# An encoder trunk on one core: the third unit of the first feed-forward layer gets two sums of weights from DRAM instead of one, and other sums are made at other times

## The chip, the core and the metric

The kernel runs on one core of one Trainium2 chip. TensorE (PE) multiplies matrices, VectorE (DVE) and ScalarE (ACT) work elementwise, GpSimd (POOL) does little here but issue adding DMAs, and SyncE (SP) issues nearly all other DMAs. The metric is the device time of one execution in microseconds (us), given as the median of several runs.

## The reference

Two layers over 256 positions of 2048 channels, all in float32. Only the feed-forward part that follows each mixer matters here:

```python
def conv_ffn(x, w_up, conv_w, conv_b, w_down):
    u = x @ w_up                                  # 2048 -> 2 * 5632, gate and value
    up = jnp.pad(u, ((0, 0), (1, 1), (0, 0)))
    u = c[0] * up[:, :-2] + c[1] * up[:, 1:-1] + c[2] * up[:, 2:] + conv_b
    gate, val = jnp.split(u, 2, axis=-1)
    return (jax.nn.silu(gate) * val) @ w_down

for layer in range(2):
    x = x + mixer(rms_norm(x))      # layer 0: pooling and attention, layer 1: mLSTM
    x = x + conv_ffn(rms_norm(x), w_up[layer], ...)
```

## The kernel before, in words

**Weights as one stream.** All weights are cut into 890 chunks of 128 x 1024 floats (512 KB), in the order in which TensorE uses them: chunks 0 to 79 for attention, 80 to 403 for the first feed-forward layer, 404 to 565 for the mLSTM layer, 566 to 889 for the second feed-forward layer. `Stream.load(i)` makes SP issue the DMA of chunk i into a buffer `w`; in a feed-forward layer it runs 7 chunks ahead of use and has 7 buffers. `Stream.split` then makes of `w` a high part, rounded by ScalarE (line 152, a cast), and a low part, the rest, by VectorE (line 153, a subtraction), both in a tile `hl`. A float32 product is three passes of TensorE: high by high, high by low, low by high. The helper that issues all of them is line 268. The order of TensorE's work is written out by hand; that of the other engines comes from a scheduler that simulates a timeline when the program is built, except for instructions that are pinned in program order.

**Units.** Of the 44 feature tiles of a feed-forward layer, 20 are made in five units of four. A unit (`quads`) multiplies with seven block products in place of eight, which needs sums of weight blocks. Call the four blocks of a pair of rows b11, b12, b22 and b21; they lie side by side in `in_q`. A unit needs b11, first = b11 + b12, second = first + b22, third = second + b21, and "left" = b12 + b22. It goes through eight pairs; each pair has two chunks early in the unit (the even one holds b11 and first, the odd one second and third) and one "left" chunk later. In `UNITS` each unit has a number that says who makes its sums:

- kind 2 (all other units): first, second and third are made in DRAM, in a tile `G`, ahead of time. SP copies b11, b22 and b21 into `G`, and POOL issues DMAs that add: b12 on b11 in two halves of 64 partitions (line 124), then first on b22 and second on b21 (line 128). SP later loads from `G`.
- kind 3 (the third unit of the first layer, before): only first is made in `G`. The odd chunk is loaded as plain b22 and b21, and VectorE makes second (line 142, `add(l, l, self.sum)`) and third (line 143, `add(r, r, l)`) in `w`, before the chunk can be split.
- "left" is made by VectorE in all of these units (line 140).

**When the sums are made.** `make_step` runs in four parts per pair, and each part hangs on the load of a chunk: `places` gives, for each pair, the chunk of part 0 and the gap between parts, so `(150 + 4 * k, 2)` puts the parts of pair k at chunks 150 + 4k, 152 + 4k and so on. Parts 0 and 1 are the two halves (SP's copies and line 124), parts 2 and 3 the two adds of line 128; kind 3 has nothing in parts 2 and 3. Five rows of `places` serve the first layer's units, and one list of 40 pairs serves the second layer's. In it `at` is 566.

A load from `G` waits on SP until the sum that it reads has landed, and holds up all loads behind it.

Of the kernel before, what the change touches and what calls it, by code (L numbers as in the profile page):

```python
# [64 lines left out]
class Stream:  # L65
# [16 lines left out]
    def load(self, pieces=1):  # L82
        i = self.n_load
        src = self.srcs[i]
        kind, src = src if isinstance(src, tuple) else ("plain", src)
        w = self.home(i, True).tile([P, CH * P], F32, tag="w", name=f"w{i}")
        if kind in ("made", "have"):
            width = n = CH * P
            at = 0
            for part in src:  # L90
                part = self.made[part[0]][:, part[1] * 512 : part[2] * 512] if isinstance(part, tuple) else part
                to = at + part.shape[-1]
                self.nc.sync.dma_start(w[:, at:to], part)
                at = to
        else:
            width = src.shape[-1]
            n = width // pieces
            for c in range(0, width, n):
                self.nc.sync.dma_start(w[:, c : c + n], src[:, c : c + n])
        self.w[i] = [w, n, width, kind, False]  # L100
        self.n_load += 1
        for step in self.make.pop(i, ()):
            self.make_step(*step)
# [7 lines left out]
    def make_step(self, key, kind, part, src):  # L111

        pin, sync, add = self.tc.keep_in_program_order, self.nc.sync, self.nc.gpsimd
        G = self.made_tile(key)
        if part < 2:
            r = slice(64 * part, 64 * part + 64)
            if kind == 1:
                pin(sync.dma_start(G[r], src[r]))
                pin(add.dma_start(G[r, 0:1024], src[r, 512:1536], accum_op=ALU.add))
            else:  # L120
                pin(sync.dma_start(G[r, 0:512], src[r, 0:512]))
                if kind == 2:
                    pin(sync.dma_start(G[r, 1024:2048], src[r, 1024:2048]))
                pin(add.dma_start(G[r, 0:512], src[r, 512:1024], accum_op=ALU.add))  # L124
        elif kind < 3:
            at = 1024 if part == 2 else 1536
            of = 0 if part == 2 else 1024
            pin(add.dma_start(G[:, at : at + 512], G[:, of : of + 512], accum_op=ALU.add))  # L128

    def sums(self, i):  # L130
        if i in self.w and not self.w[i][4] and self.w[i][3] not in ("plain", "made"):
            w, kind = self.w[i][0], self.w[i][3]
            l, r = w[:, 0:512], w[:, 512:1024]
            pin, add = self.tc.keep_in_program_order, self.nc.vector.tensor_add
            if kind == "sum":
                pin(add(r, r, l))
            if kind in ("sum", "have"):
                self.sum = r
            if kind == "left":
                pin(add(l, l, r))  # L140
            if kind == "chain":
                pin(add(l, l, self.sum))
                pin(add(r, r, l))
            self.w[i][4] = True
# [30 lines left out]
class Weave:  # L175
# [6 lines left out]
    def add(self, gen, delay=0.0):  # L182
        self.q.append([self.t + delay, gen])
# [37 lines left out]
def trunk(ctx: ExitStack, tc: tile.TileContext, gx, xT, xn, call, catt, cml, weights, make, out):  # L221
# [716 lines left out]
    def ffn_layer(layer, norm, nxt):  # L938
        with ExitStack() as es:
# [199 lines left out]
            def sums_ready():  # L1139
                yield from wv.wait(lambda: norm.R is not None)  # L1140
                v.tensor_scalar_mul(n0, norm.rcol[:, 0:1], -1.0)
                yield from sums()
# [82 lines left out]
def _down_chunks(w):  # L1225
# [6 lines left out]


UNITS = (
    ((1, 1, 17, 38, 2), (2, 1, 45, 64, 2), (3, 1, 71, 97, 3), (4, 1, 104, 127, 2), (5, 1, 134, 157, 2)),
    ((1, 1, 17, 39, 2), (2, 1, 46, 67, 2), (3, 1, 74, 97, 2), (4, 1, 104, 128, 2), (5, 1, 135, 157, 2)),
)

# [1 line left out]
def _ffn_plan(layer):  # L1240

    slots = []
    for c, n in enumerate(FCH):
        fill = [("n", c, i) for i in range(n) if not any(u[0] == c and u[1] == i // 4 for u in UNITS[layer])]
        if c:
            per = len(fill) // NB
            fill = sum(([*fill[per * b : per * b + per], ("d", c - 1, b)] for b in range(NB)), [])
            if c == 2 and any(u[:2] == (1, 1) for u in UNITS[layer]):
                fill = [fill[i] for i in (0, 2, 1, 4, 3, 6, 5, 7)]
        for e in fill:  # L1250
            slots += [e] * (4 if e[0] == "n" else FCH[e[1]] // 2)
    here = [[] for _ in slots]
    m = KT // 2
    for c, h, lo, hi, _ in UNITS[layer]:
        one, two = 2 * m, m + m // 2
        step = (hi - lo - 3) / (one + two)
        for k in range(one + two):
            here[int(lo + k * step + (3 if k >= one else 0))].append(("s", c, h))
    plan = []
    for e, extra in zip(slots, here):  # L1260
        plan += [e] + extra
    for b in range(NB):
        plan += [("d", len(FCH) - 1, b)] * (FCH[-1] // 2)
    return plan
# [15 lines left out]
def _ffn_order(layer, up, dn, four, last):  # L1280

    pos, seq = {}, []
    m = KT // 2
    d0 = [sum(FCH[:c]) // 2 * NB for c in range(len(FCH))]
    for step in _ffn_plan(layer):
        kind, c, i = step
        n = pos.get(step, 0)
        pos[step] = n + 1
        if kind == "n":
            seq.append(up[(sum(FCH[:c]) + i) * 4 + n])  # L1290
        elif kind == "d":
            seq.append(dn[d0[c] + i * (FCH[c] // 2) + n])
        else:
            u = [e[:2] for e in UNITS[layer]].index((c, i))
            made = UNITS[layer][u][4]
            if n >= 2 * m and (n - 2 * m) % 3 == 2:
                seq.append(last[u, (n - 2 * m) // 3])
                continue
            at = n // 2 if n < 2 * m else (n - 2 * m) // 3 * 2 + (n - 2 * m) % 3
            q, key = four[u, at], f"{layer}{c}{i}_{at}"  # L1300
            if n >= 2 * m:
                seq.append(("made", ((key, 1, 2), q[:, 1024:1536])) if made == 1 else ("left", q[:, 512:1536]))
            elif n % 2:
                seq.append(("made", ((key, 2, 4),)) if made in (1, 2) else ("chain", q[:, 1024:2048]))
            else:
                seq.append((("made", "have")[made == 3], (q[:, 0:512], (key, 0, 1))) if made else ("sum", q[:, 0:1024]))
    return seq
# [124 lines left out]
```

## Time and profile before

| | us |
|---|---|
| median of 3 runs | 2164.64 (2164.61 to 2164.88) |
| the profiled execution | 2164.07 |
| its span, first to last instruction | 2162.3 |
| PE busy | 2155.0 |
| DVE busy | 1716.1 |
| ACT busy | 1308.5 |
| POOL busy | 276.0 |

The mean granted TensorE clock is 0.999 of full speed, and the DMAs move 276 GB/s on average. A row of the profile names the line, the engine, the tile written and those read, a count, the busy time and the mean of one; a row of the waits names who waited, for what, the sum in us, how often, and the longest one. A row of the timeline gives start and duration in us, and in brackets the idle time before it with what ended it. SPq stands for the issuing of DMAs by SP.

### The profile page before, as it was taken

How to read it: one execution, taken by the hardware profiler on the slowest of the kernel's cores; microseconds unless marked ns; L12 is line 12 of the kernel's file. 1: busy time of each engine (PE TensorE's matmuls, PEld its weight loads, DVE VectorE, ACT ScalarE, POOL GpSimd, SP SyncE). 2: the span in 40 equal slices, each digit the busy share in tenths (PEclk: the TensorE clock that was granted, in tenths of full speed). 3: DMA queues.
4: the chain of work that ended last, by engine and by line, in shares of the span. 5: the costliest groups of instructions: out<-in, count | busy, mean ns of one | idle time of the engine just before them, and what ended most of it. 6: DMA issues, size and time to landing. Idle time of an engine off the chain costs nothing.

```text
span 2162.3 us, 31058 instructions
## 1 busy us (share of the span) xinstructions
PE 2155.0 (100%) x10896; PEld 1827.3 (85%) x10896; DVE 1716.1 (79%) x2400; ACT 1308.5 (61%) x1840; POOL 276.0 (13%) x344
## 2 busy tenths in 40 slices
PE   9999999999999999999999999999999999999999
PEld 7888888888888888889888888888888888888887
DVE  7686698989888797866777676669898888879785
ACT  7665566766556576656554544456676666757663
POOL 0222111211111111101111111110000000000000
PEclk9999999999999999999999999999999999999999
DMA  9878899999999999979899988877999999877773
GB/s 327 256 226 247 253 262 329 336 329 315 311 328 297 360 312 348 315 207 249 250 268 247 259 249 247 259 243 223 312 284 309 301 294 291 272 253 235 260 244 119
DMA packets 204702, 596.15 MB, mean 276 GB/s; under 512 B 26010, under 2 KB 28354, under 8 KB 204546
## 3 DMA queue, kind: packets, MB, share of 16 engines
q1 hardware_dynamic: 167776, 531.43, 70.1%
q0 software_dynamic: 33696, 59.00, 18.6%
q10 hardware_dynamic: 3074, 3.75, 0.9%
q8 instruction: 85, 1.39, 0.2%
q14 instruction: 71, 0.58, 0.1%
HBM read 591.93 MB, written 119.58 MB: 329 GB/s over the span
## 4 chain that ended last, share of the span: by engine, by line
PE 99%; DVE 1%; issue 0%; ACT 0%; DVEq 0%; ACTq 0%
PE up L268 25%; PE dn L268 21%; PE p L268 17%; PE op L268 8%; PE mv L268 4%; PE mk L268 4%; PE mq L268 4%; PE mo L268 4%; PE qproj L268 3%; PE kproj L268 1%; PE pool L268 1%; PE vproj L268 1%; PE tr L1081 1%; PE av L268 1%; PE qk L268 1%; PE end L268 1%
## 5 line engine op out<-in xcount | busy, mean ns | idle before, releaser
L153 DVE TENSOR_TENSOR hl<-w,hl 128x1024 fp32r<-128x1024 f32 (+2 forms) x892 | 1074.0, 1217 | 323.0 <-ACT hl L152 309.0
L152 ACT CAST hl<-w 128x1024 fp32r<-128x1024 f32 (+2 forms) x891 | 923.5, 1048 | 641.3 <-PE dn L268 105.0
L268 PE MATMUL up<-xx,hl 128*128 128x512 f32 (+1 forms) x3072 | 560.7, 337 | 0.0
L268 PEld LDWEIGHTS up<-xx,hl 128*128 128x128 f32 x3072 | 486.8, 188 | 76.7
L268 PE MATMUL dn<-hl,g 128*128 128x512 f32 x2064 | 492.0, 391 | 0.0
L268 PEld LDWEIGHTS dn<-hl,g 128*128 128x128 f32 x2064 | 386.1, 188 | 79.4
L268 PE MATMUL p<-hl,sx 128*128 128x512 f32 x960 | 250.4, 390 | 1.9 <-DVE hl L153 1.9
L124 POOL DMA_DIRECT2D G<-in_q x160 | 132.1, 827 | 881.0 <-DMA G<-in_q 877.4
L268 PEld LDWEIGHTS p<-hl,sx 128*128 128x128 f32 x960 | 175.9, 188 | 36.6 <-DVE hl L153 2.9
L128 POOL DMA_DIRECT2D G<-G x144 | 127.3, 884 | 530.7 <-DMA G<-in_q 228.2
L268 PE MATMUL p<-hl,xx 128*128 128x512 f32 x720 | 193.7, 391 | 0.0
L268 PEld LDWEIGHTS p<-hl,xx 128*128 128x128 f32 x720 | 131.1, 188 | 24.2
L268 PE MATMUL mk<-xx,hl 128*128 128x512 f32 (+1 forms) x512 | 92.5, 338 | 0.0
L268 PE MATMUL mq<-xx,hl 128*128 128x512 f32 (+1 forms) x512 | 92.2, 337 | 0.0
L268 PE MATMUL mv<-hl,xx 128*128 128x512 f32 (+2 forms) x480 | 91.7, 350 | 0.0
L268 PE MATMUL op<-hl,cat 128*128 128x512 f32 x384 | 91.6, 393 | 0.0
L268 PE MATMUL mo<-hl,xx 128*128 128x512 f32 x384 | 90.5, 391 | 0.0
L268 PE MATMUL op<-hl,mcat 128*128 128x512 f32 x384 | 89.5, 392 | 0.0
L268 PEld LDWEIGHTS mq<-xx,hl 128*128 128x128 f32 x512 | 79.3, 188 | 11.6
L268 PEld LDWEIGHTS mk<-xx,hl 128*128 128x128 f32 x512 | 79.0, 188 | 11.7 <-DVE hl L153 0.4
L268 PEld LDWEIGHTS mv<-hl,xx 128*128 128x128 f32 x480 | 78.3, 189 | 11.2
L268 PEld LDWEIGHTS op<-hl,mcat 128*128 128x128 f32 x384 | 71.5, 188 | 14.6
(242 smaller groups left out, 1861.5 us busy)
## 6 DMA issues: line engine op xcount, KB each, us to landing
w<-in_up SPq DMA_DIRECT2D x192, 512.0 KB, 6.2
w<-in_dn SPq DMA_DIRECT2D x176, 512.0 KB, 6.1
w<-in_m_in SPq DMA_DIRECT2D x124, 512.0 KB, 5.9
w<-in_q SPq DMA_DIRECT2D x88, 512.0 KB, 6.3
G<-in_q SPq DMA_DIRECT2D x144, 256.0 KB, 6.5
G<-G POOLq DMA_DIRECT2D x144, 256.0 KB, 7.5
w<-G SPq DMA_DIRECT2D x72, 512.0 KB, 6.5
w<-in_a_in SPq DMA_DIRECT2D x46, 512.0 KB, 6.1
```

The lines of the kernel that those rows point to most:

```text
L124: pin(add.dma_start(G[r, 0:512], src[r, 512:1024], accum_op=ALU.add))
L128: pin(add.dma_start(G[:, at : at + 512], G[:, of : of + 512], accum_op=ALU.add))
L152: (self.nc.vector.tensor_copy if i + c == 0 else self.nc.scalar.copy)(hl[:, 0, c : c + n], w[:, c : c + n])
L153: self.nc.vector.tensor_sub(hl[:, 1, c : c + n], w[:, c : c + n], hl[:, 0, c : c + n].bitcast(F32))
L268: pe.matmul(out_, lhsT, rhs, start=start, stop=stop, skip_group_check=True)
L1081: pe.transpose(tr[:, j, t * P : t * P + P], src[:, c : c + P], ident)
```

## The change

A new kind 4: first and second are made in `G`, third is left to VectorE. The third unit of the first layer goes from kind 3 to kind 4. Its even chunk is loaded as before. Its odd chunk ("half") is loaded in two pieces, second from `G` and b21 from `in_q`, and VectorE adds once. `places` of this unit, of the fourth unit of the first layer, and of the first 28 pairs of the second layer change: 4 of these 28 pairs, not 7, start before the end of the first feed-forward layer, and 24, not 21, run along the mLSTM layer.

```diff
@@ Stream.load
-        if kind in ("made", "have"):
+        if kind in ("made", "have", "half"):
@@ Stream.make_step
                 pin(sync.dma_start(G[r, 0:512], src[r, 0:512]))
-                if kind == 2:
-                    pin(sync.dma_start(G[r, 1024:2048], src[r, 1024:2048]))
+                if kind in (2, 4):
+                    to = 2048 if kind == 2 else 1536
+                    pin(sync.dma_start(G[r, 1024:to], src[r, 1024:to]))
                 pin(add.dma_start(G[r, 0:512], src[r, 512:1024], accum_op=ALU.add))
-        elif kind < 3:
+        elif kind < 3 or kind == 4 and part == 2:
@@ Stream.sums
             if kind in ("sum", "have"):
                 self.sum = r
+            if kind == "half":
+                pin(add(r, r, l))
@@ UNITS
-    (... (3, 1, 71, 97, 3), ...),
+    (... (3, 1, 71, 97, 4), ...),
@@ _ffn_order
             elif n % 2:
-                seq.append(("made", ((key, 2, 4),)) if made in (1, 2) else ("chain", q[:, 1024:2048]))
+                seq.append(("half", ((key, 2, 3), q[:, 1536:2048])) if made == 4 else
+                           ("made", ((key, 2, 4),)) if made in (1, 2) else ("chain", q[:, 1024:2048]))
@@ kernel
-              + [(150 + 4 * k, 2) for k in range(8)] + [(180 + 10 * k, 5) for k in range(8)]
+              + [(148 + 5 * k, 2) for k in range(8)] + [(192 + 9 * k, 5) for k in range(8)]
-    places.append([(at - 240 + 11 * k, 5) for k in range(7)] + [(at - 162 + 38 * k // 5, 4) for k in range(21)]
+    places.append([(at - 220 + 14 * k, 5) for k in range(4)] + [(at - 164 + 20 * k // 3, 4) for k in range(24)]
```

More of the change, by code (lines that the diff above doesn't have):

```diff
@@ L1234 @@
 UNITS = (
-    ((1, 1, 17, 38, 2), (2, 1, 45, 64, 2), (3, 1, 71, 97, 3), (4, 1, 104, 127, 2), (5, 1, 134, 157, 2)),
+    ((1, 1, 17, 38, 2), (2, 1, 45, 64, 2), (3, 1, 71, 97, 4), (4, 1, 104, 127, 2), (5, 1, 134, 157, 2)),
     ((1, 1, 17, 39, 2), (2, 1, 46, 67, 2), (3, 1, 74, 97, 2), (4, 1, 104, 128, 2), (5, 1, 135, 157, 2)),
```

## The prediction

> **What bounds the kernel now.** I read the page's busy times first, then TensorE's own waits, then the timeline around the one wait found, then the stretches of DMA.
>
> ```profile
> span 2162.3 us, 31058 instructions
> ...
> PE 2155.0 (100%) x10896; PEld 1827.3 (85%) x10896; DVE 1716.1 (79%) x2400; ACT 1308.5 (61%) x1840; POOL 276.0 (13%) x344
> ```
>
> TensorE is busy for all but 7.3 us of the span, and its order and amount of work are not touched. So only a wait that goes, or a new one, can move the time. The view of waits, for TensorE alone, has two rows in the whole execution:
>
> ```profile
> PE p L268 <- DVE hl L153: 1.9, 1, 1.9
> PE wps L292 <- DVE pad L661: 1.2, 1, 1.2
> ```
>
> The second is the start of the program. The first is a product of a unit (p) that waited for the low part of its weights. The timeline of TensorE and that of VectorE show it at 570.83 us:
>
> ```profile
> 568.55 0.39 PE L268 MATMUL p<-hl,sx 128*128 128x512 f32 x1
> 570.83 0.73 PE L268 MATMUL p<-hl,sx 128*128 128x512 f32 x2 [1.89 <-DVE hl L153]
> ```
>
> ```profile
> 562.76 0.68 DVE L142 TENSOR_TENSOR w<-w,w 128x512 f32<-128x512 f32 x1
> ...
> 565.29 0.68 DVE L143 TENSOR_TENSOR w<-w 128x512 f32<-128x512 f32 x1
> ...
> 566.69 2.35 DVE L153 TENSOR_TENSOR hl<-w,hl 128x1024 fp32r<-128x1024 f32 x2
> 568.96 0.68 DVE L142 TENSOR_TENSOR w<-w,w 128x512 f32<-128x512 f32 x1
> 569.56 1.22 DVE L153 TENSOR_TENSOR hl<-w,hl 128x1024 fp32r<-128x1024 f32 x1
> ```
>
> The subtraction that TensorE needed ran from 569.56 to 570.78, and TensorE went on at 570.83. VectorE was busy without a break before it, and two adds of line 142 and one of line 143 stand in that stretch. These lines run only in the unit of kind 3, the one that is changed. The wait has a second price, in the clock column of the view by stretches (the third from the end: granted clock, then DMA share, then GB/s):
>
> ```profile
> core 0: us, PE busy (x) PEld busy (x) DVE busy (x) ACT busy (x) POOL busy (x), PEclk, DMA share, GB/s
> 568.00:570.00 2.00, 0.94 (x5) 0.44 (x3) 2.00 (x3) 0.35 (x2) 1.08 (x2) 1.00 1.04 394
> 570.00:572.00 2.00, 1.17 (x4) 0.99 (x5) 2.00 (x4) 0.62 (x2) 0.53 (x1) 0.89 1.07 312
> 572.00:575.00 3.00, 3.00 (x8) 2.32 (x8) 2.18 (x3) 1.86 (x2) 0.00 (x0) 0.51 1.00 247
> ```
>
> After the wait the clock fell to half until 575: 2 us x 0.11 + 3 us x 0.49 = 1.69 us of TensorE's time were lost.
>
> **The change part by part.** First the prices of one multiplication and of one chunk's time, from the chain that ended last:
>
> ```profile
> 261.55 4.91 PE up L268 x28
> ...
> 977.22 12.24 PE mv L268 x96
> ...
> 2103.67 43.53 PE dn L268 x192
> ```
>
> 43.53 us / 192 = 0.227 us from one multiplication to the next when nothing waits. From 568.55 to 570.83 is 2.28 us, so the wait cost 2.28 - 0.23 = 2.05 us, and with the clock 2.05 + 1.69 = 3.74 us. The first feed-forward layer takes its 324 chunks from 261.55 to 977.22, 2.21 us each.
>
> *VectorE's adds.* Groups of the whole execution:
>
> ```profile
> L140 DVE TENSOR_TENSOR w<-w x80: 678/683/692, 359.1 to 2069.8; 128x512 f32<-128x512 f32 x80
> ```
>
> ```profile
> L143 DVE TENSOR_TENSOR w<-w 128x512 f32<-128x512 f32 x8 | 5.5, 684 | 0.1
> L142 DVE TENSOR_TENSOR w<-w,w 128x512 f32<-128x512 f32 x8 | 5.5, 683 | 0.0
> ```
>
> The sixteen adds of the odd chunks become eight, each as long as one of line 143: 8 x 0.683 = 5.5 us less on VectorE in this unit. What that takes off the wait is bounded from below by the adds of line 142 in the busy stretch, 2 x 0.68 = 1.36 us, and from above by the whole 2.05 us. I take the whole: the odd chunk then looks like a "left" chunk, one add before its split, and 80 of those in ten units (line 140) gave TensorE no wait. If only 1.36 us went, 0.7 us and perhaps some clock would stay.
>
> *More DMAs for unit three.* Per pair SP copies b22 in two more DMAs, POOL issues one more adding DMA (line 128), and the odd chunk is loaded by two DMAs in place of one (line 93). Their issue times, minimum/median/maximum in ns:
>
> ```profile
> L93 SPq DMA_DIRECT2D w<-G x152: 326/334/1096, 280.9 to 2015.2; - x152
> L123 SPq DMA_DIRECT2D G<-in_q x144: 496/584/2829, 51.1 to 1849.3; - x144
> L128 POOL DMA_DIRECT2D G<-G x144: 812/824/1167, 73.6 to 1864.6; - x144
> ```
>
> SP: 8 x (2 x 0.584 + 0.334) = 12.0 us of issuing; POOL: 8 x 0.824 = 6.6 us. Both hide: SP stands waiting for free buffers most of the time, and POOL is busy 276 of 2162 us. Behind a waiting add on POOL stand only other adds, and the powers of the normalisations (below).
>
> The bytes are the larger matter. Eight pairs move 256 KB more by SP and 256 KB more by POOL, 4.19 MB. The steps of the fourth unit move away in exchange: counted over the parts that hang on chunks 148 to 189, the sums' traffic goes from 5376 to 8448 KB, 3.15 MB more; over chunks 148 to 403 it is even (39424 to 39680 KB). Chunk 148 is used near 261.6 + 68 x 2.21 = 412 us and loaded 7 chunks earlier, 396 us; chunk 189 likewise near 487 us. The view by stretches:
>
> ```profile
> 325.00:400.00 75.00, 75.00 (x375) 63.26 (x374) 62.23 (x76) 46.07 (x55) 12.13 (x15) 1.00 1.04 340
> 400.00:490.00 90.00, 90.00 (x452) 76.25 (x451) 80.93 (x113) 62.90 (x86) 17.44 (x22) 1.00 1.01 323
> ...
> 700.00:840.00 140.00, 140.00 (x689) 118.19 (x688) 116.91 (x147) 88.92 (x112) 25.84 (x32) 1.00 1.04 343
> 976.00:1372.00 396.00, 396.00 (x2179) 343.30 (x2179) 279.36 (x454) 204.22 (x277) 62.58 (x78) 1.00 0.90 250
> ```
>
> 3.15 MB in 90 us are 35 GB/s, so the stretch would ask for 323 + 35 = 358 GB/s. The DMAs gave 343 GB/s for 140 us from 700 on, with a full TensorE. Lower end of the cost: 0, since the loads run 7 chunks, some 15 us, ahead. Upper end: if 343 is all there is, the loads fall (358 - 343) x 90 / 343 = 3.9 us behind by 490 us, and if all of it reaches TensorE, with the clock's 1.69 us, 5.6 us. I take 0, because ScalarE already waits for late landings between 700 and 840 us while TensorE has no gap there:
>
> ```profile
> ACT hl L152 <- DMA w<-in_up: 7.6, 7, 1.7
> ACT hl L152 <- DMA w<-G: 5.9, 6, 1.9
> ```
>
> If that cover were gone, each late microsecond would be TensorE's.
>
> *Moved steps.* A part's sum must land before the chunk that loads it. In unit three the closest is now 48 chunks ahead, in unit four 24 (29 before), in the second layer far over 100 as before; 24 x 2.21 = 53 us. So none is late, and SP, in order, is not held. From 320 to 403 the first layer loses 3840 KB, and the mLSTM layer gains 3840 KB, 10 issues on SP and 10 on POOL: 3.93 MB over 396 us are 10 GB/s on 250. The cover is large; without it the price is the last rival's. From both sides: 0 to that price; I take 0.
>
> *The sum.* Profiled execution 2164.07 - 3.74 = 2160.33 us. The median of the runs is 0.57 us above it, so 2160.9 us as a median, 0.17% less. The measurement tells about 0.2%, 4.3 us, from no change: this gain falls just short, and no other wait is left to take away.
>
> The Trainium skill, "TensorE: Matmul & The Clock Gate", Part 1, says that the array falls to half clock after at least one idle window of some 3.4 us. By it a wait of 1.89 us would not lower the clock; here the clock fell right behind it (0.51), so the trace does not agree. By that rule the 1.69 us would have another cause and stay: the second rival.
>
> **The rivals.**
>
> 1. *A wait stays in unit three.* The scheduler writes VectorE's order anew; a subtraction may again stand behind others. For: VectorE has no break from 562.76 to 570.78. Against: 5.5 us less work there. With the 0.7 us above and the clock's loss left, 2164.64 - 1.36 = 2163.3 us; with all of it left, 2164.6 us.
> 2. *The half clock stays without the wait.* Then only 2.05 us go: 2162.6 us. Against: the clock is 1.00 in every other stretch quoted here.
> 3. *The DMAs become the bound from 396 to 490 us (slower).* For: 358 GB/s asked, and the stretch before it, 325 to 400, already has a DMA share of 1.04, so there is no rest between the two. Against: the even stretch of 140 us. It decides from the point at which the loads are later than the 15 us they run ahead, less their landing time. Price at most 5.6 us: 2160.9 + 5.6 = 2166.5 us, slower than before, though within 0.2%. Two such waits would pass 0.2%.
> 4. *POOL's queue holds up the mLSTM layer.* The powers of its normalisation stand between the adds on POOL; one waited:
>
> ```profile
> POOL ry_h L275 <- DMA w<-in_m_in: 8.7, 1, 8.7
> ```
>
> It cost TensorE nothing. If a new one did in full: 2160.9 + 8.7 = 2169.6 us.
>
> That the change does not do what it says would need a sum in `G` that comes late, which the distances exclude.
>
> **How the numbers follow.** Chances: the forecast 0.69 (its own range 2160.2 to 2161.6), a wait that stays 0.11, the half clock that stays 0.03, the DMAs 0.12, POOL 0.05. The range runs from 2160.2 to 2165.0: it takes in the first two rivals and a third of the third one's price range. Faster by over 0.2% (below 2160.3) 0.07, the lower edge of the forecast; slower by over 0.2% (above 2169.0) 0.05, from POOL and from two waits on the DMAs; within 0.2% 0.88.
>
> **What would show it.** Right: the waits of TensorE have no row with p left, the clock shows 1.00 at 568 to 576 us, line 142 is gone and one add of eight stands in its place, DVE's busy time is 5 to 6 us lower, the GB/s between 400 and 490 us are near 350. Wrong: a row "PE ... <- DVE hl" at another place, or ScalarE's waits for landings between 400 and 490 us with gaps of TensorE behind them.

## The result, and the profile after

The change made the kernel slower: 2169.92 us against 2164.37 us (medians of 21 runs each), a ratio of 1.0026 with an interval of 1.0020 to 1.0033. That is 5.6 us more, where the prediction had 3.7 us less and a range that ended at 2165.0. The profiled execution of the changed kernel took 2166.15 us, near the lowest of its 21 runs (2166.13), so its trace shows less of the loss than the median. Line numbers after the changed functions are higher by three: 152, 153 and 268 are now 155, 156 and 271.

The page of the changed kernel, its busy times:

```profile
span 2164.4 us, 31111 instructions
...
PE 2154.4 (100%) x10896; PEld 1826.5 (84%) x10896; DVE 1712.1 (79%) x2392; ACT 1309.3 (60%) x1840; POOL 283.6 (13%) x352
```

VectorE has eight instructions less and is 4.0 us less busy, POOL has the eight adding DMAs more. The eight adds that are left stand at line 141, in the view of groups:

```profile
L141 DVE TENSOR_TENSOR w<-w 128x512 f32<-128x512 f32 x8 | 5.5, 688 | 0.0
```

TensorE's waits in the whole execution (who waited, for what: sum in us, times, longest):

```profile
PE p L271 <- ACT hl L155: 1.9, 1, 1.9
PE p L271 <- DVE hl L156: 1.7, 2, 0.9
PE wps L295 <- DVE pad L664: 1.2, 1, 1.2
PE mk L271 <- DVE hl L156: 1.1, 1, 1.1
```

Before there was one row besides the start. Now there are three. None of them stands at 570 us. The stretches (us, busy time of PE, PEld, DVE, ACT and POOL with counts, granted clock, DMA share, GB/s) show where they are:

```profile
400.00:490.00 90.00, 87.18 (x437) 73.37 (x436) 74.20 (x104) 59.20 (x82) 18.50 (x23) 1.00 1.04 321
490.00:520.00 30.00, 29.13 (x141) 23.86 (x140) 26.41 (x31) 18.43 (x21) 4.02 (x5) 1.00 1.02 351
565.00:576.00 11.00, 11.00 (x51) 9.09 (x50) 9.02 (x13) 5.69 (x7) 1.64 (x2) 1.00 1.03 331
976.00:1372.00 396.00, 394.86 (x2178) 342.58 (x2177) 277.93 (x451) 203.16 (x277) 72.92 (x91) 1.00 0.92 258
```

At 565 to 576 us TensorE is full and the clock is 1.00: the old wait and its half clock are gone. From 400 to 490 TensorE lost 2.8 us, from 490 to 520 another 0.9, and in the mLSTM layer 1.1 us. In the stretch that was to get 3.15 MB more, the DMAs moved 321 GB/s, no more than the 323 before, at a share of 1.04 in place of 1.01. More was asked of them, and they gave no more. What that did to the loads' lead shows in SP's waits in this stretch, before and then after:

```profile
SPq L99 <- DVE hl L153: 28.8, 18, 3.0
```

```profile
SPq L99 <- DVE hl L156: 5.5, 6, 2.4
```

In these rows SP has the next load ready and waits until VectorE has split a chunk and so freed a buffer: the loads are as far ahead as the buffers allow. With all rows of the view, SP stood 48.9 of the 90 us for an engine and 9.9 us for DMAs before; after, it stood 10.5 and 43.4 us.

The timeline around 482 us, ScalarE first and then TensorE, has the whole chain:

```profile
481.63 1.99 ACT L155 CAST hl<-w 128x1024 fp32r<-128x1024 f32 x2 [3.32 <-DMA w<-in_dn]
```

```profile
483.67 0.50 PE L271 MATMUL p<-hl,sx 128*128 128x512 f32 x1 [1.87 <-ACT hl L155]
485.12 1.43 PE L271 MATMUL p<-hl,sx 128*128 128x512 f32 x5 [0.95 <-DVE hl L156]
```

A plain chunk (`in_dn`) landed late, ScalarE stood 3.32 us for it, the cast behind it ended only at 483.62 us, and TensorE ran out of split weights, first of the high part, then of the low one. ScalarE's waits from 400 to 520 us show that it was not one chunk:

```profile
ACT hl L155 <- DMA w<-G: 11.0, 7, 3.2
...
ACT hl L155 <- DMA w<-in_up: 5.8, 6, 1.5
ACT hl L155 <- DMA w<-in_dn: 4.5, 5, 3.3
...
ACT hl L155 <- DMA w<-in_b: 2.7, 2, 2.1
```

Twenty loads of four kinds were late, 24.0 us in sum. In the kernel before, the same view has no row in which ScalarE waited for a landing. That is the sign that the prediction named for its being wrong: ScalarE waiting for landings there, with gaps of TensorE behind them.

The third row of the waits belongs to the start of the mLSTM layer. VectorE's timeline there, then TensorE's:

```profile
1015.43 0.35 DVE L832 SCALAR_TENSOR_TENSOR arg<-G,mc,kml 128x128 f32<-128x128 f32 x1 [1.40 <-DMA G<-gd]
1017.43 1.15 DVE L832 SCALAR_TENSOR_TENSOR arg<-G,mc,kml 128x256 f32<-128x256 f32 x3 [1.66 <-DMA G<-gd]
...
1019.09 1.22 DVE L156 TENSOR_TENSOR hl<-w,hl 128x1024 fp32r<-128x1024 f32 x1
```

```profile
1020.37 0.97 PE L271 MATMUL mk<-xx,hl 128*128 128x256 f32 x4 [1.15 <-DVE hl L156]
```

VectorE takes its instructions in order. It stands for the small DMAs of the gates (`G<-gd`; this `G` is a tile of the gates, not one of the sums), and the split that TensorE needs next is queued behind. Before, it stood there as well, up to 2.79 us at a time, but at 1015.12 us had the last of it, 2.3 us sooner, and TensorE went through.

### The profile page after: what moved, and what is told of

It reads as the page before. It is cut to its first block, busy times and chain, and to the rows that moved or that the text cites. A ratio compares the mean times of both kernels' runs of the same rounds, so it can differ in the third digit from the quotient of the medians.

```text
span 2164.4 us, 31111 instructions
## 1 busy us (share of the span) xinstructions
PE 2154.4 (100%) x10896; PEld 1826.5 (84%) x10896; DVE 1712.1 (79%) x2392; ACT 1309.3 (60%) x1840; POOL 283.6 (13%) x352
## 4 chain that ended last, share of the span: by engine, by line
PE 92%; DMA 5%; DVE 2%; issue 1%; ACT 0%; SPq 0%; ACTq 0%; DVEq 0%
PE up L271 22%; PE dn L271 20%; PE p L271 16%; PE op L271 8%; PE mo L271 4%; PE mk L271 4%; PE mq L271 4%; PE mv L271 4%; PE qproj L271 3%; DMA G<-in_q 1%; PE kproj L271 1%; PE pool L271 1%; PE vproj L271 1%; DVE hl L156 1%; DMA w<-in_up 1%; DMA w<-G 1%
## 5 line engine op out<-in xcount | busy, mean ns | idle before, releaser
L129 POOL DMA_DIRECT2D G<-G x152 | 145.6, 958 | 387.4 <-DMA G<-in_q 158.5
```

## The experiments

Each kernel was timed in five rounds. Those of one group ran on one chip and share the runs of the kernel before; the groups ran on different chips. Where two kernels of a group are compared, the difference is that of the means of their runs, with a 95% interval from the spread of those runs.

| kernel | median us | before | ratio and interval |
|---|---|---|---|
| *first group* | | 2163.94 | |
| a: one add, no other change | 2160.28 | | 0.9986 (0.9978 to 0.9995) |
| c: changed, second layer's list as before | 2166.39 | | 1.0014 (1.0005 to 1.0023) |
| d: before, second layer's list as changed | 2164.71 | | 1.0004 (0.9995 to 1.0013) |
| e: as c, sums of unit three far earlier | 2164.63 | | 1.0008 (0.9999 to 1.0017) |
| *second group* | | 2163.76 | |
| f: as c, second sum made but not used | 2170.20 | | 1.0042 (1.0028 to 1.0055) |
| g: second sum for three pairs, from chunk 82 | 2161.84 | | 0.9990 (0.9981 to 0.9999) |
| h: five pairs' sums early, three late | 2168.29 | | 1.0022 (1.0013 to 1.0031) |
| the changed kernel again | 2172.68 | | 1.0039 (1.0026 to 1.0052) |
| *third group* | | 2163.85 | |
| i: as g, from chunk 54 | 2160.54 | | 0.9986 (0.9977 to 0.9995) |
| j: as i, second layer's list as changed | 2161.45 | | 0.9993 (0.9984 to 1.0002) |
| l: second sum for three pairs, at the old times | 2163.14 | | 0.9998 (0.9989 to 1.0007) |

**a. VectorE's saving alone.** The kernel before without one of the two adds; the DMAs stay as they were. Left out: first is not added to b22.

```diff
             if kind == "chain":
-                pin(add(l, l, self.sum))
                 pin(add(r, r, l))
```

> The kernel before, but VectorE makes one add of the two per odd chunk of unit three (first is not added to b22, so the sums of this unit are not the reference's); every DMA and its time as before. Theory DMA (the 4.2 MB that kind 4 adds between 396 and 490 us make landings late, and that is what costs): the wait at 570 us goes and nothing comes, 3.7 us under the kernel before, near 2160.7 us. Theory order (the scheduler's new order on VectorE, not the DMAs, makes the new waits): 2168 us or more, with waits of TensorE near 483 and 512 us. Theory mLSTM (the 24 sums along the mLSTM layer cost most of it): 2160.7 us.

0.9986, 3.7 us less by the medians. TensorE's waits, and the stretch from 400 to 490 us:

```profile
PE wps L291 <- DVE pad L660: 1.2, 1, 1.2
```

```profile
400.00:490.00 90.00, 90.00 (x452) 76.22 (x451) 80.67 (x112) 62.90 (x86) 17.40 (x22) 1.00 1.01 320
```

Only the start's row is left. By the means it is 3.4 us (2.5 to 4.3), so the eight adds are worth about what the prediction gave them. VectorE's order without them brings no wait by itself.

**c. The first layer's part of the change without the second layer's.**

```diff
 (the change, but)
-    places.append([(at - 220 + 14 * k, 5) for k in range(4)] + [(at - 164 + 20 * k // 3, 4) for k in range(24)]
+    places.append([(at - 240 + 11 * k, 5) for k in range(7)] + [(at - 162 + 38 * k // 5, 4) for k in range(21)]
```

> The changed kernel, but the sums of the second layer at their times of before (7 and 21). Theory DMA: the waits at 480 to 515 us stay and those of the mLSTM layer go, some 1 to 2 us under the changed kernel, 2167 to 2169 us. Theory order: the same as the changed kernel, 2169 to 2170 us. Theory mLSTM: most of the loss goes, 2161 to 2163 us, and 480 to 515 us has little wait.

1.0014. TensorE's wait and the stretch:

```profile
PE p L271 <- DVE hl L156: 1.5, 2, 0.9
```

```profile
400.00:490.00 90.00, 88.97 (x444) 74.76 (x443) 76.47 (x107) 60.04 (x83) 19.45 (x24) 1.00 1.04 328
```

The waits stand at 483 and 511 us, none in the mLSTM layer. So the first layer alone turns the gain into a loss: c less a, 6.3 us (4.7 to 8.0), is what unit three's DMAs cost, together with the moved times of units three and four. The profiled execution is the fastest of c's 11 (2162.68 us) and shows only 1.7 us of TensorE's time lost from 400 to 520 us; the second profile of the changed kernel, below, shows more.

**d. The second layer's part alone.** The edit to `places` above the other way round, on the kernel before.

> The kernel before with only the times of the second layer's sums changed (4 and 24). Theory DMA: one more wait of 1 to 2 us near 1020 us, 2165 to 2167 us, and the wait at 570 us stays. Theory order: as before, 2164.4 us. Theory mLSTM: 2168 to 2170 us.

1.0004, an interval that holds 1. The profile has the old wait and no other of TensorE's besides the start:

```profile
PE p L268 <- DVE hl L153: 1.9, 1, 1.9
```

**e. The same sums, far earlier.** As c, with unit three's four parts under attention and unit four's as before.

```diff
-              + [(148 + 5 * k, 2) for k in range(8)] + [(192 + 9 * k, 5) for k in range(8)]
+              + [(26 + 13 * k // 2, 3) for k in range(8)] + [(180 + 10 * k, 5) for k in range(8)]
```

> Kind 4 in unit three, but its sums are made along the attention layer, at chunks 26 + 13k/2, where the DMAs move 230 to 280 GB/s; units four and the second layer at their times of before. Theory DMA: no late landing between 396 and 490 us, no wait at 570 us, 2160.7 to 2161.5 us, faster than both. Theory order: the new waits on VectorE stay, 2167 us or more. Theory mLSTM: 2161 us.

1.0008: no gain, but for another reason. The stretch, TensorE's largest wait and VectorE's timeline before it:

```profile
400.00:490.00 90.00, 90.00 (x455) 76.33 (x454) 80.30 (x110) 62.92 (x86) 5.58 (x7) 1.00 0.85 279
```

```profile
PE ov L271 <- ACT pt L571: 1.4, 1, 1.4
```

```profile
154.48 0.43 DVE L675 TENSOR_TENSOR pad<-w,inv 128x256 f32<-128x256 f32 x1 [4.68 <-DMA inv<-in_catt]
```

The feed-forward layer has no wait left, with the same kind of sums as in c: the waits there come from the bytes in that stretch, not from the kind. But the sums now run beside attention, whose DMA of `inv` lands 7.7 us after its issue (5.1 before); VectorE stood 4.68 us for it (2.14 before), and TensorE waited at 160 us. Behind that wait the clock was 0.66 from 160 to 165 us, another 5 x 0.34 = 1.7 us. By the times alone e is not told apart from c (c less e is 1.1 us, -1.2 to 3.3) and costs 5.2 us (3.3 to 7.2) over a; that the loss changed its place is read from the traces.

**f. The DMAs without VectorE's saving.** The odd chunk loaded plain and added twice as before, while the second sum is still made in `G` and read by nobody.

```diff
-                seq.append(("half", ...) if made == 4 else
+                seq.append(... ("chain", q[:, 1024:2048]))
-                seq.append((("made", "have")[made == 3], ...
+                seq.append((("made", "have")[made in (3, 4)], ...
```

> The DMAs of kind 4 without its gain: second is made in DRAM for unit three at the changed times of units three and four (second layer's list as before), but the odd chunk is loaded and summed as in the kernel before, so second in DRAM goes unused. Theory DMA: both losses, the wait of 570 us or its like and the late landings at 400 to 520 us, ScalarE waiting 15 to 25 us for landings there; 2168 to 2171 us. Theory late half (not the amount of DMA, but the odd chunk in two pieces and its load from the sum is what comes late): no wait at 480 to 515 us, 2164.4 us as before.

1.0042, beside 1.0039 for the changed kernel on this chip; f less the kernel before is 7.4 us (4.0 to 10.8). TensorE's waits for `p`:

```profile
PE p L271 <- DVE hl L156: 3.8, 3, 2.1
...
PE p L271 <- ACT hl L155: 0.8, 2, 0.6
```

The old wait (2.1 us, at 576 us) is back, this time with the clock at 1.00 behind it, and the ones near 484 and 512 us are there too, though no chunk of unit three is loaded in halves. Late landings come from the traffic, not from the split load.

**g. Fewer sums, and early.** In before's profile only one odd chunk came late. So pairs 3, 4 and 5 alone get the second sum, the others stay of kind 3; the three pairs' sums are made from chunk 82 on.

```diff
+def kind_of(made, p):
+    return 4 if made == 3 and p in (3, 4, 5) else made
...
-              + [(150 + 4 * k, 2) for k in range(8)]
+              + [(82 + 6 * (k - 3), 3) if k in (3, 4, 5) else (150 + 4 * k, 2) for k in range(8)]
```

> Kind 4 for pairs 3, 4 and 5 of unit three alone, their sums at chunks 82, 88 and 94, loaded between 260 and 300 us where the DMAs have room; the other five pairs as before, and all other times as before. Theory DMA: three adds of line 142 go, those in front of the late subtraction, and 396 to 490 us moves 1.6 MB less than before: no wait at 570 and none at 480 to 515 us, 2160.5 to 2161.5 us. Theory order: a new order on VectorE costs something somewhere, 2164 us or more.

0.9990. The wait at 570 us is gone and none came in its place there; one of 1.1 us at 268 us is new, behind POOL. VectorE's timeline:

```profile
265.66 0.16 DVE L280 TENSOR_TENSOR re_n<-ry_n 128x2 f32<-128x2 f32 x1 [3.20 <-POOL ry_n L278]
```

**h. All eight pairs, five of them early.**

```diff
-              + [(148 + 5 * k, 2) for k in range(8)]
+              + [(78 + 5 * k, 2) if k < 5 else (158 + 8 * (k - 5), 3) for k in range(8)]
```

> Kind 4 for all of unit three, the sums of pairs 0 to 4 at chunks 78 to 98, five apart, and of pairs 5 to 7 at 158, 166 and 174; all other times as before. Theory DMA: between 396 and 490 us 1 MB less than in the kernel before, 2160.5 to 2161.5 us if the stretch from 255 to 310 us holds 5 MB more; where it does not, waits of TensorE between 300 and 400 us. Theory order: 2166 us or more with waits near 483 and 512 us.

1.0022, and nearly all of it from one place. POOL's timeline, VectorE's, TensorE's, and the stretch with the wait's end:

```profile
265.99 1.66 POOL L129 DMA_DIRECT2D G<-G  x2 [5.41 <-DMA G<-in_q]
267.05 1.42 POOL L125 DMA_DIRECT2D G<-in_q  x1
267.58 1.63 POOL L278 TENSOR_TENSOR ry_n<-rv_n,mhalf 128x2 f32<-128x2 f32 x1
```

```profile
258.85 0.17 DVE L276 TENSOR_SCALAR rv_n<-nsum 128x2 f32<-128x2 f32 x1
...
269.25 0.16 DVE L280 TENSOR_TENSOR re_n<-ry_n 128x2 f32<-128x2 f32 x1 [7.97 <-POOL ry_n L278]
```

```profile
269.86 0.96 PE L271 MATMUL up<-xx,hl 128*128 128x512 f32 x4 [4.45 <-DVE xx L337]
```

```profile
269.00:280.00 11.00, 9.13 (x35) 7.64 (x36) 10.75 (x21) 6.00 (x9) 3.80 (x6) 0.69 0.84 152
```

The normalisation's power `ry_n` was ready to run from 259 us on, but POOL's queue held it behind an adding DMA that itself stood 5.41 us for a copy. The wait has a second price, a clock of 0.69 from 269 to 280 us: 11 x 0.31 = 3.4 us. Together 4.45 + 3.4 = 7.9 us, which fits the time: h is 4.3 us (3.5 to 5.1) above the kernel before, though it saves VectorE's 3.4 us. This is the prediction's fourth rival, in another layer. In the changed kernel itself it does not occur.

**The changed kernel again**, with a profile (2169.75 us) near the median of its first 21 runs.

> The changed kernel once more, beside the others on one chip, for a second profiled execution: its first one was the fastest of 21 (2166.1 us against a median of 2169.9). Theory DMA: a slower execution shows the same places, 480 to 515 us and the start of the mLSTM layer near 1020 us, with longer waits; 2168 to 2171 us. Theory mLSTM: a slower execution shows several waits between 976 and 1372 us that the first one had not.

1.0039. TensorE's waits and two stretches:

```profile
PE p L271 <- ACT hl L155: 1.5, 1, 1.5
PE mk L271 <- DVE hl L156: 1.4, 1, 1.4
PE p L271 <- DVE hl L156: 1.4, 2, 0.9
...
PE up L271 <- DVE hl L156: 0.9, 2, 0.5
```

```profile
400.00:490.00 90.00, 86.09 (x425) 70.80 (x425) 73.83 (x102) 57.02 (x80) 18.74 (x24) 1.00 1.03 310
488.00:495.00 7.00, 6.63 (x22) 5.27 (x23) 6.54 (x11) 3.12 (x5) 0.00 (x0) 0.76 1.02 305
```

The same places, more of each: waits from 461 us on, 310 GB/s, and this time the clock fell after the waits at 487 and 488 us, 7 x 0.24 = 1.7 us. With the 3.9 us of idle TensorE from 400 to 490 us that makes 5.6 us in this one place, close to the 6.3 us of c less a. The first profile had no such fall of the clock, which accounts for part of the distance between that profile and the median: of the first 21 runs, the seven with a mean clock of 1.000 took 2168.2 us in the mean, the four with 0.998 took 2171.8.

**i. The three pairs, earlier still**, from chunk 54, so that no part of them hangs on a chunk near the normalisation at 260 us.

```diff
-  (82 + 6 * (k - 3), 3) if k in (3, 4, 5)
+  (54 + 7 * (k - 3), 3) if k in (3, 4, 5)
```

> Kind 4 for pairs 3, 4 and 5 of unit three alone, as in the run with chunks 82 to 94, but their sums at chunks 54, 61 and 68, done before the normalisation whose power stands on POOL near 260 us; all other times as in the kernel before. Theory POOL queue (what was left at 268 us in that run was the power of the normalisation behind POOL's waiting adds): no wait at 268, 480 to 515 or 570 us, 2160.3 to 2161.0 us. Theory order: some wait stays, 2161.8 us or more.

0.9986, the best kernel of the study: it beats the kernel before by 3.3 us (medians), and by its ratio the changed one (1.0026) too. TensorE's waits and the stretch:

```profile
PE wps L295 <- DVE pad L664: 1.2, 1, 1.2
PE ov L271 <- DVE pt L572: 0.4, 1, 0.4
```

```profile
400.00:490.00 90.00, 90.00 (x452) 76.26 (x451) 79.32 (x110) 62.73 (x86) 12.69 (x16) 1.00 0.94 303
```

It gains what a gains, though it computes everything.

**j. i with the second layer's list of the change.**

```diff
-    places.append([(at - 240 + 11 * k, 5) for k in range(7)] + [(at - 162 + 38 * k // 5, 4) for k in range(21)]
+    places.append([(at - 220 + 14 * k, 5) for k in range(4)] + [(at - 164 + 20 * k // 3, 4) for k in range(24)]
```

> The same, with the changed times of the second layer's sums (4 and 24). Theory thin place (at the start of the mLSTM layer VectorE waits for the gates' DMA, and more traffic there makes TensorE wait near 1020 us): 1 to 3 us above the run without, 2161.5 to 2163.5 us. Theory knock-on (the wait at 1020 us comes only with the late loads of the first feed-forward layer): the same as the run without, within 0.7 us.

0.9993; j less i is 1.3 us (-0.1 to 2.7). TensorE's row, and VectorE's between 990 and 1030 us:

```profile
PE mk L271 <- DVE hl L156: 1.9, 1, 1.9
```

```profile
DVE arg L832 <- DMA G<-gd: 5.5, 2, 2.8
```

The wait of the mLSTM layer (at 1016 us) is here without any wait in the feed-forward layer. So it is not a consequence of those, as "knock-on" had it: it comes with the moved sums alone, though not always, since d has them and no such wait. Behind it the clock was 0.76 from 1016 to 1023 us, another 1.7 us; this execution (2163.49 us) is 2.0 us above j's median.

**l. The three pairs at the old times.** As i, with `places` as before.

```diff
-  (54 + 7 * (k - 3), 3) if k in (3, 4, 5) else (150 + 4 * k, 2)
+  (150 + 4 * k, 2)
```

> Kind 4 for pairs 3, 4 and 5 of unit three alone, all sums at the times of the kernel before, so 1.6 MB more between 396 and 490 us. Theory DMA (the loss grows with the bytes added there): a third of the waits of the 4.2 MB, 0.5 to 2 us between 460 and 515 us, the wait at 570 us gone, 2161 to 2163 us. Theory order: as the changed kernel without its second layer's times, 2166 us.

0.9998; l less i is 2.3 us (1.4 to 3.3), for the same instructions and bytes at another time. TensorE's waits and the stretch:

```profile
PE p L271 <- DVE hl L156: 2.0, 2, 1.0
...
PE p L271 <- ACT hl L155: 1.1, 2, 0.9
```

```profile
400.00:490.00 90.00, 88.04 (x440) 74.03 (x439) 75.63 (x105) 60.69 (x83) 18.30 (x23) 1.00 1.03 319
```

Against the kernel before, l has 3 x 0.52 = 1.57 MB more in the stretch, and i has 1.57 MB less. As a has the traffic of before and gains what i gains, I put the 2.3 us down to l's 1.57 MB above that level; the change has 3.15 MB above it and costs 6.3 us (c less a). That is an estimate of 1.5 and 2.0 us for each MB. A MB takes 3.1 us at 320 GB/s, so half to two thirds of its transfer time reached TensorE.

## Why the prediction was wrong

- **VectorE's adds: right.** 3.74 us were forecast; a shows 3.7 by its medians, 3.4 (2.5 to 4.3) by its means. Line 142 is gone, the clock is 1.00 at 568 to 576 us, DVE's busy time fell by 4.0 us (5 to 6 forecast). The first two rivals, a wait or a half clock that stays at 570 us, did not come.
- **"More DMAs for unit three", taken as 0: wrong. This is the step that failed.** It measured 6.3 us (4.7 to 8.0), around or above its upper end of 5.6. The rival that described it, the DMAs as the bound from 396 to 490 us, had a chance of 0.12 and a price too small. Three links of its working failed. First, what the DMAs can give: 343 GB/s from 700 to 840 us was carried over to another stretch. From 400 to 490 they gave 310 to 328 in the five profiles with a share of 1.03 or 1.04 there (the changed kernel twice, c, f and l), 15 to 33 less. Against the 358 asked for, 321 would leave the loads (358 - 321) x 90 / 321 = 10 us behind by the prediction's own formula, not 3.9. The Trainium skill, "DMA: Bandwidth & Descriptors", Specifications, gives some 358 GB/s as a core's share of the memory. By that figure the request would just have fitted; these runs got 310 to 328, and none shows what held them below it. Second, the cover. "Loads run 7 chunks ahead" counts only while the lead is full. 325 to 400 us before it ran at 1.04 already, and in the stretch itself SP's 48.9 us of standing for an engine, the sign of a full lead, fell to 10.5. Third, the argument from 700 to 840 us, that ScalarE waits for landings there without a gap of TensorE. It shows that lateness can be hidden, not how much is still free, and ScalarE's sum does not tell: it waited 14.4 us for loads from 400 to 520 us in l, where TensorE lost 3.1 us, and 14.0 us from 325 to 400 us in the kernel before, where TensorE lost nothing. It may be that only some late chunks count: in c, f, l and the first profile of the changed kernel the waits stand at the same two places, near 483 and 512 us; why there stays open.
- **"Moved steps", taken as 0: wrong on the second layer's part, in size small.** The new wait near 1016 to 1024 us appears in three of the four profiles with the new list (the changed kernel twice, and j, but not d) and in none of the nine with the old one. The list's price is 0.6 us (-0.4 to 1.6; d less before) to 1.3 us (j less i); each of these intervals holds 0, so that it costs anything is shown by the traces more than by the times. Why d is spared is open. VectorE's wait for `G<-gd` alone doesn't decide it, since before and i have that too; what differs is which splits stand behind it.
- **POOL's queue: a real mechanism, at another place.** It cost 4.45 us in h, and 3.4 us more by the clock. That POOL's 13% of busy time hides the adds was no argument: what is held up there is held by waiting, not by work.
- **The sum, made anew with the measured sizes:** -3.4 (a less before, by the means) + 6.3 (c less a) + 0.6 to 1.3 (the list) = 3.5 to 4.2 us, against 5.6 us (4.3 to 7.1) for the whole change. The two agree within their uncertainty; a further microsecond or two, if they are there, are not placed. Theories that fell: "order", since a, e and i have new orders of VectorE's work and no wait in the feed-forward layer; "late half", by f; "mLSTM", that the second layer's list costs most, by c and d; "knock-on", by j.

## What to carry to other kernels

A sum moved from an engine to the memory is paid in DMA time: in a stretch that already ran at a DMA share of 1.01, each MB added cost an estimated 1.5 to 2.0 us here, and the GB/s of another stretch were no guide to what it would give. A share of 1.0 does not by itself mean a loss: i's sums raised it from 0.91 to 1.02 between 180 and 262 us without a wait there. So look also at how long SP stands for buffers that an engine must free, which shows the lead: from 400 to 490 us it was 48.9 us before, 30.4 in l and 10.5 after the change. Make such sums only for the chunks that come late (three of eight gave the whole gain), and keep them away from DMAs that an engine is about to wait for and from computing on the queue that issues them.

## What the runs showed of the hardware

- At a DMA share of 1.03 or 1.04 the GB/s differ widely by stretch: 284 from 180 to 220 us (i), 310 to 328 from 400 to 490 us (five profiles), 343 from 700 to 840 us (before), 363 from 490 to 520 us (the changed kernel again). The share does not tell the rate.
- The clock falls to about half after some of TensorE's waits of 1.4 to 2.1 us and not after others, whether or not a shorter wait follows. It fell behind 1.89 us (before), 1.36 and 0.53 us (e), 1.95 us (j) and 1.55 and 0.95 us (the changed kernel again), and each fall lost 1.7 us; behind 4.45 us (h) it lost 3.4 us. It did not fall behind 1.87 and 0.95 us (the first profile of the changed kernel) or 2.06 us (f). "TensorE: Matmul & The Clock Gate" of the Trainium skill, Part 1, says that the window that decides runs freely and doesn't start with the kernel, which would allow such differences; that it takes an idle window of 3.4 us does not agree with the falls behind the shorter waits.
- A normalisation of two numbers per partition on POOL, 1.6 us long, came 8.6 us late behind one waiting adding DMA (h).
